# Twelve weight units of the second layer's token mixer get their lo part from an accumulating DMA and a negated ScalarE write

## The chip, the cores and the metric

One core of one Trainium2 chip runs the whole program. The metric is the device time of one execution in microseconds (us); the lower the better.

## What is computed

The reference is a decoder trunk of two layers over 256 tokens of width 1024, in float32. Each layer is a token mixer (one input projection of the normed activations, from which a latent attention, a second attention and a gated convolution are fed, then gates and an output projection) and a channel mixer:

```
z = h @ w_in
...
q_a = (rms_norm(q_lat, mla_q_norm_g) @ w_uq)...
kv = (rms_norm(kv_lat, mla_kv_norm_g) @ w_ukv)...
...
u = glu_a * jax.nn.sigmoid(glu_g)
u = causal_depthwise_conv(u, conv_dw_w, conv_dw_b)
u = jax.nn.silu(layer_norm(u, conv_ln_g, conv_ln_b))
...
merged = g[:, :, 0] * o_a + g[:, :, 1] * o_b + g[:, :, 2] * o_c
return merged @ w_out
```

In layer 2 (index 1 in the code) the change touches columns of `w_in` (those of the second attention's query, key and value, here called QKV, and those of the convolution's input, here called C) and the two up-projections `w_uq` (UQ) and `w_ukv` (UK).

## The kernel before

**Weights in units.** The weights stream from HBM in units of 128 x 1024 float32 (512 KB; 128 x 768 for UQ). SyncE (SP) issues one DMA for each into a tile `raw`, of which there are four (`wload`, L204). Every product is made from two parts of each operand: `hi`, the operand rounded to the matmul's fp32r type, and `lo`, the rest. `split` (L221 to L233) makes them for a weight unit: ScalarE copies `raw` into `hi` (tile `whi`, L231), and VectorE subtracts, `lo = raw - hi` (tile `wlo`, L232). There are four buffers of `whi` and of `wlo` as well. An activation's two parts are named `hh`/`hl`, `qlh`/`qll`, `klt` and so on.

**Three matmuls a product.** A product is hi times hi (L315), activation lo times weight hi (L316), activation hi times weight lo (L318). `flush` (L304) writes out a group of queued products: first the L315 and L316 matmuls of them all, then all the L318 matmuls. So `wlo` is needed only towards the end of a group; this last part is called phase 3 below. `take` (L280) keeps three units split ahead of the one in use. So `wlo` is written before the matmuls that come to need it.

**Order of the work.** The steps of a layer stand in a list written by hand (`STEPS`), one token for a step; a unit belongs to the step's token, and its load, its `hi` and its `lo` are written into the program when `take` draws it, three units ahead. Every engine then carries out its own instructions in the order in which the program's scheduler put them; the tiles rotate as they come free. SP's DMA queue is in order too: a load whose `raw` buffer isn't yet released holds up the loads behind it. The units of layer 2's mixer come in this order: QKV00, QKV01, the three of UQ (UQ0, UQ1, UQ2), QKV02, the two of UK (UK0, UK1), QKV03, QKV10 to QKV13, QKV20 to QKV23, C00, C01, C10, C11, C20, C21, then gate units (G) with C30 and C31 among them. Here QKVab is the b-th quarter of the inputs for the a-th of query, key, value, and Cab the b-th half for the a-th group of channels.

**What else runs there.** `proj_qkv` (L965) uses the QKV units one at a time. `up_q` (L987) takes all three UQ units and uses them in four groups of products; `up_kv` (L1002) takes the two UK units and does the same. Ahead of `up_q` ScalarE copies the latents out of PSUM (L926, L927, L929) and squares them (L938) for their norm. VectorE has, besides the subtractions, the 31 taps of the depthwise convolution in four groups of channels (L1141, `cacc`), spread over the steps from the first of the QKV group to the last of the second attention's steps, and the work on the attentions' queries and keys. After the last tap come the mean (a matmul on TensorE, L1154, tile `psb`) and its subtraction (L1159). GpSimd (POOL) does small powers for the norms (`rstd_of`, L536), and nothing else there.

Of the kernel before, what the change touches and what calls it, by code (L numbers as in the profile page):

```python
# [9 lines left out]
F32 = mybir.dt.float32  # L10
# [3 lines left out]
AF = mybir.ActivationFunctionType  # L14
ALU = mybir.AluOpType
# [42 lines left out]
LEAD = 16  # L58

LEADS = {(0, "O", 6): 0, (0, "G", 7, 0): 40, (1, "G", 6, 0): 0, (1, "O", 4): 40}  # L60
# [98 lines left out]
def trunk_kernel(ctx, tc, xT, crow, ccol, pos, invf, modb_d, cols_d, grow_d, wmh, wmr, wm, win1, wqkv,  # L159
                  wgc, wgab, wuq, wukv, woab, woc, wout, wup, wdn, out):  # L160
    nc = tc.nc
    te, ac, ve, gp, sy = nc.tensor, nc.scalar, nc.vector, nc.gpsimd, nc.sync
# [8 lines left out]
    def nm(s):  # L171
        uid[0] += 1
        return f"{s}_{uid[0]}"
# [27 lines left out]
    def wload(src, tag="raw", bufs=4):  # L201
        n = src.shape[1]
        t = wk.tile([P, 1024], F32, tag=tag, name=nm("raw"), bufs=bufs, align_bytes=LINE if tag != "raw" else None)
        sy.dma_start(t[:, 0:n], src)  # L204
        return t[:, 0:n]
# [11 lines left out]
    def wload_unit(src):  # L217
        loads[0] += 1
        return wload(src, *raw_tags[loads[0] % len(raw_tags)])

    def split(raw, lead):  # L221
        n = raw.shape[1]
        turn[0] += 1
        th, nh = hi_tags[turn[0] % len(hi_tags)]
        tl, nl = lo_tags[turn[0] % len(lo_tags)]
        hi, lo = (wk.tile([P, 1024 + 128], F32R, tag=t, name=nm(m), bufs=b, align_bytes=LINE)[:, lead:lead + n]
                  for t, m, b in ((th, "whi", nh), (tl, "wlo", nl)))
        with ExitStack() as es:
            for i in (pins.pop(0) if pins else hold[0] or []):
                es.enter_context(tc.issue_after(i))  # L230
            ac.activation(hi, raw, AF.Copy)  # L231
            ve.tensor_tensor(lo, raw, hi.bitcast(F32), op=ALU.subtract)  # L232
        return hi, lo  # L233

    def chop(src, n, c, size=1024):

        m = max(1, size // c)
        return [(src[:, k0 * c:min(n, k0 + m) * c], range(k0, min(n, k0 + m))) for k0 in range(0, n, m)]

    def token_units(l, t):  # L240

        if t[0] == "KL":
            return [(win1[l, t[1], :, 0:672], [0])]
        if t[0] == "QKV":
            return [chop(wqkv[l, t[1], t[2] // 2], 4, 512)[t[2] % 2]]
        if t[0] in ("UQ", "UK"):
            return chop(wuq[l], 3, 768) if t[0] == "UQ" else chop(wukv[l], 2, 1024)
        if t[0] in ("C", "G"):
            return [chop((wgc if t[0] == "C" else wgab)[l, t[1]], KD, S)[t[2]]]
        if t[0] == "O":  # L250
            return chop(woab[l, t[1]], 1, 1024)
        if t[0] == "OC" and t[1] % 2 == 0:
            return chop(woc[l, t[1] // 2], 1, 1024)
        if t[0] == "PR" and t[1] % 2 == 0:
            return chop(wout[l, t[1] // 2], 2, 1024)
        return []

    def all_units():
        for l in range(L):
            for k in range(KD):  # L260
                if l == 0:
                    yield win1[l, k, :, 0:672], [0], LEAD
                yield win1[l, k, :, 672:1696], [0], LEAD
            for t in CFG["order"][l]:
                yield from ((*u, LEADS.get((l, *t), LEAD)) for u in token_units(l, t))
            if l == 1:
                for first in (0, NRAW):
                    for i in range(2):
                        for j in range(first, first + NRAW):
                            yield *chop(wup[l, j], KD, S)[i], LEAD  # L270
            for up, j in FFN[l]:
                if up and l == 1 and j < 2 * NRAW:
                    continue
                for i, u in enumerate(chop(wup[l, j], KD, S) if up else chop(wdn[l, j], 1, 1024)):
                    yield *u, (0, 40)[i] if up and j in PAIRS else LEAD

    ahead = [AHEAD0]
    coming, ready = list(all_units())[::-1], []

    def take(n=1):  # L280

        while coming and len(ready) < n + ahead[0]:
            src, ks, lead = coming.pop()
            ready.append((split(wload_unit(src), lead), src.shape[1] // len(ks), ks))
        res = []
        for _ in range(n):
            (hi, lo), c, ks = ready.pop(0)
            res.append([(k, (hi[:, i * c:(i + 1) * c], lo[:, i * c:(i + 1) * c])) for i, k in enumerate(ks)])
        return res

    def take1():
        return take()[0][0][1]
# [486 lines left out]
    def layer(l):  # L779
# [65 lines left out]
        def pair(name, part, bank=psb):  # L845

            if part == 0:
                pairs[name] = bank()
            for k, w in take()[0]:
                cols2(pairs[name], w, k, k == 0, k == KD - 1)  # L850
            flush()
            return pairs[name]
# [114 lines left out]
        def proj_qkv(i, q):  # L967
            if q == 0:
                pqkv[i] = [psa() if i < 2 else psb() for _ in range(2)]
            pp = pqkv[i]  # L970
            for kk, w in take()[0]:
                k = 4 * (q // 2) + kk
                for b in range(NB):
                    rows(pp[b], w, k, b, k == 0, k == KD - 1)
            flush()
            if q < 3:
                return
            for b in range(NB):
                if i < 2:
                    if qks[b] is None:  # L980
                        qks[b] = mq()
                    ac.activation(qks[b][:, i * 512:(i + 1) * 512], pp[b], AF.Copy)
                else:
                    ac.activation(vb[:, b, :], pp[b], AF.Copy)
# [569 lines left out]
```

## Time and profile before

| what | value |
|---|---|
| runs of the kernel | 904.81, 904.56 and 902.16 us, median 904.56 us |
| the profiled execution | 905.91 us |
| its span, first to last instruction | 903.7 us |
| mean granted TensorE clock | 0.994 |
| weight units split | 286 |
| DMA traffic | 201.59 MB |

The profiled execution is 1.35 us above the median of the runs; the rest of its time beside the span, 2.2 us, lies ahead of the first and behind the last instruction. In the rows of the profile PE is a matmul on TensorE, PEld its weight load, DVE is VectorE, ACT is ScalarE, POOL is GpSimd and SP is SyncE. A row of a timeline is the start in us, the duration, the engine, the line, the operation, the tiles, and in brackets the idle time of the engine ahead of it with what ended it. In a row of groups the figures behind the first bar are busy us and mean ns of one instruction, and behind the second bar the idle time. Matmuls are pipelined, so a row's duration overlaps that of the next; how far apart rows start tells the pace.

### The profile page before, as it was taken

To read this page: it belongs to the slowest core of one execution; us is meant where nothing else is said; L and a number is where in the kernel's file an instruction comes from. 1 tells how busy PE (TensorE), PEld (TensorE's weight loads), DVE (VectorE), ACT (ScalarE), POOL (GpSimd) and SP (SyncE) were. 2 spreads that over 40 slices of the span, in tenths; PEclk is the share of its full clock that TensorE was granted. 3 is DMA by queue.
4 is the path that set the end of the run, shared out by engine and by line. 5 is a ranking of instruction groups with operands and counts; after the bars stand their busy time and mean duration, and the time that the engine had idled before them with its cause. 6 is when DMAs were issued, how large, how long until landed. Compare 5 with 4: busy or idle time off the path is not lost.

```text
span 903.7 us, 18611 instructions
## 1 busy us (share of the span) xinstructions
PE 884.4 (98%) x7247; PEld 839.6 (93%) x7247; DVE 808.1 (89%) x1592; ACT 559.3 (62%) x998; POOL 47.0 (5%) x36
## 2 busy tenths in 40 slices
PE   8999999999999999999999999999999999999998
PEld 6888888999997999999989988989999999999998
DVE  6989999999987999999774999999987899998774
ACT  4677588644755655556543676787465777556551
POOL 1010700000000000000000033000000000000000
PEclk8999999999999999999999999999999999999999
DMA  8956535699888889996652666156866576886631
GB/s 320 375 202 205 187 118 175 207 330 316 309 285 286 288 287 314 316 306 228 204 161 77 200 196 200 49 167 230 274 200 209 160 233 188 301 280 205 191 95 47
DMA packets 57976, 201.59 MB, mean 223 GB/s; under 512 B 6944, under 2 KB 8480, under 8 KB 57888
## 3 DMA queue, kind: packets, MB, share of 16 engines
q1 hardware_dynamic: 57888, 200.41, 66.5%
q8 instruction: 57, 0.93, 0.4%
q14 instruction: 31, 0.25, 0.1%
HBM read 199.33 MB, written 1.05 MB: 222 GB/s over the span
## 4 chain that ended last, share of the span: by engine, by line
PE 78%; DVE 11%; DMA 5%; ACT 3%; issue 2%; SPq 0%; POOL 0%; DVEq 0%; ACTq 0%; POOLq 0%
PE psb L315 16%; PE psb L316 15%; PE psb L318 15%; PE psa L315 8%; PE psa L316 8%; PE psa L318 8%; DVE wlo L232 3%; DVE cacc L1141 2%; ACT whi L231 1%; DVE raw L816 1%; PE psa L423 1%; PE psa L734 1%; PE psa L746 1%; DMA raw<-in_win 1%; DMA raw<-in_wmh 1%
## 5 line engine op out<-in xcount | busy, mean ns | idle before, releaser
L231 ACT ACTIVATE whi<-raw 128x1024 fp32r<-128x1024 f32 (+2 forms) x286 | 296.0, 1042 | 194.4 <-PE psb L316 98.5
L232 DVE TENSOR_TENSOR wlo<-raw,whi 128x1024 fp32r<-128x1024 f32 (+2 forms) x286 | 340.3, 1195 | 50.7 <-ACT whi L231 42.4
L315 PE MATMUL psb<-hh,whi 128*128 128x256 f32 x1056 | 256.0, 282 | 0.5 <-ACT p L713 0.3
L316 PE MATMUL psb<-hl,whi 128*128 128x256 f32 x1056 | 253.7, 280 | 0.0
L315 PEld LDWEIGHTS psb<-hh,whi 128*128 128x128 f32 x1056 | 198.9, 189 | 5.0 <-issue 2.6
L316 PEld LDWEIGHTS psb<-hl,whi 128*128 128x128 f32 x1056 | 199.0, 189 | 0.5 <-DVE wlo L232 0.4
L318 PE MATMUL psb<-hh,wlo 128*128 128x256 f32 x1056 | 145.0, 279 | 0.0
L318 PEld LDWEIGHTS psb<-hh,wlo 128*128 128x128 f32 x1056 | 131.7, 188 | 0.8 <-issue 0.8
L1141 DVE SCALAR_TENSOR_TENSOR cacc<-upad,cw,cacc 128x256 f32<-128x256 f32 x240 | 105.8, 478 | 0.4
L315 PE MATMUL psa<-mhl,whi 128*128 128x256 f32 x400 | 94.2, 278 | 0.0
L316 PE MATMUL psa<-mhl,whi 128*128 128x256 f32 x400 | 94.0, 278 | 0.0
L1423 DVE SCALAR_TENSOR_TENSOR e<-psb,fw,e 128x255 f32<-128x255 f32 (+1 forms) x168 | 80.0, 478 | 6.6 <-ACT e L1421 6.0
L536 POOL TENSOR_TENSOR rs<-rs,mhalf 128x8 f32<-128x8 f32 (+3 forms) x26 | 45.5, 1761 | 678.0 <-DVE rs L535 677.9
L315 PEld LDWEIGHTS psa<-mhl,whi 128*128 128x128 f32 x400 | 75.1, 188 | 0.0
L316 PEld LDWEIGHTS psa<-mhl,whi 128*128 128x128 f32 x400 | 75.0, 188 | 0.0
L406 DVE SCALAR_TENSOR_TENSOR raw<-raw,crow 128x1024 f32<-128x1024 f32 x56 | 68.3, 1220 | 0.9 <-DMA raw<-in_wmr 0.9
L1421 ACT ACTIVATE e<-psb,fb,fw 128x256 f32<-128x256 f32 x84 | 46.5, 554 | 23.6 <-DVE e L1423 20.1
L318 PE MATMUL psa<-mhl,wlo 128*128 128x256 f32 x400 | 54.0, 278 | 0.0
L318 PEld LDWEIGHTS psa<-mhl,wlo 128*128 128x128 f32 x400 | 49.5, 188 | 0.0
L1431 ACT ACTIVATE mhl<-e 128x256 fp32r<-128x256 f32 x44 | 18.4, 417 | 39.7 <-DVE e L1429 38.0
L315 PE MATMUL psb<-whi,hh 128*128 128x416 f32 (+1 forms) x96 | 30.9, 350 | 2.9 <-ACT hh L892 2.9
L315 PE MATMUL psa<-hh,whi 128*128 128x256 f32 x128 | 30.0, 281 | 0.0
(295 smaller groups left out, 1522.2 us busy)
## 6 DMA issues: line engine op xcount, KB each, us to landing
raw<-in_wup SPq DMA_DIRECT2D x88, 512.0 KB, 4.9
raw<-in_wmr SPq DMA_DIRECT2D x68, 512.0 KB, 5.4
raw<-in_wdn SPq DMA_DIRECT2D x44, 512.0 KB, 4.6
raw<-in_wgab SPq DMA_DIRECT2D x32, 512.0 KB, 5.0
raw<-in_wqkv SPq DMA_DIRECT2D x24, 512.0 KB, 4.7
raw<-in_wm SPq DMA_DIRECT2D x24, 512.0 KB, 4.7
raw<-in_win SPq DMA_DIRECT2D x16, 512.0 KB, 4.5
raw<-in_wgc SPq DMA_DIRECT2D x16, 512.0 KB, 4.4
```

The costliest lines, as they stand in the source:

```text
L231: ac.activation(hi, raw, AF.Copy)
L232: ve.tensor_tensor(lo, raw, hi.bitcast(F32), op=ALU.subtract)
L315: te.matmul(o, p1[0], p1[1], start=start, stop=False)
L316: te.matmul(o, p2[0], p2[1], start=False, stop=False)
L318: last = te.matmul(o, p3[0], p3[1], start=False, stop=stop)
L406: ve.scalar_tensor_tensor(raw, raw, scale, row, op0=ALU.mult, op1=ALU.mult, accum_out=acc)
L423: te.matmul(acc[32 * c:32 * c + 32, 0:S], cact[:, k:k + 1].to_broadcast([P, 32]), raw[:, c * S:(c + 1) * S], start=(k == 0), stop=(k == KD ...
L536: gp.tensor_tensor(r, r, mhalf[:, :n], op=ALU.pow)
L1141: ve.scalar_tensor_tensor(aj, upad[:, j, t:t + S], cw[:, j * 31 + t:j * 31 + t + 1], aj, op0=ALU.mult, op1=ALU.add)
L1421: ac.activation(t, src, AF.Identity, scale=fw[:, 2, c:c + 1], bias=fb[:, c:c + 1])
L1423: ve.scalar_tensor_tensor(t[:, d:S], src[:, 0:S - d], fw[:, 2 - d, c:c + 1], t[:, d:S], op0=ALU.mult, op1=ALU.add)
L1431: ac.activation(mh, th, AF.Copy)
```

## The change

For twelve units of layer 2's mixer (UQ1, UK1 and those of QKV and C with an odd second index: QKV01, QKV03, QKV11, QKV13, QKV21, QKV23, C01, C11, C21, C31), `lo` is made in another way. ScalarE writes minus the rounded weight into `lo` (`activation` with scale -1); GpSimd issues a DMA from `raw` to `lo`, which adds what it reads to what stands there; and ScalarE then writes `hi` as before. VectorE has no part in it. The other 274 units are made as before. The result is the same `lo`, and the matmuls are the same. Lines behind the first edit move by 5 to 9 (L318 becomes L327, L938 becomes L947).

```diff
-    def split(raw, lead):
+    def split(raw, lead, added=False):
...
-            ac.activation(hi, raw, AF.Copy)
-            ve.tensor_tensor(lo, raw, hi.bitcast(F32), op=ALU.subtract)
+            if added:
+                ac.activation(lo, raw, AF.Copy, scale=-1.0)
+                gp.dma_start(lo, raw, accum_op=ALU.add)
+                ac.activation(hi, raw, AF.Copy)
+            else:
+                ac.activation(hi, raw, AF.Copy)
+                ve.tensor_tensor(lo, raw, hi.bitcast(F32), op=ALU.subtract)
...
+    def added(l, t, i):
+
+        return l == 1 and (t[0] in ("UQ", "UK") and i % 2 == 1 or t[0] in ("QKV", "C") and t[2] % 2 == 1)
...
-                yield from ((*u, LEADS.get((l, *t), LEAD)) for u in token_units(l, t))
+                yield from ((*u, LEADS.get((l, *t), LEAD), added(l, t, i)) for i, u in enumerate(token_units(l, t)))
...
-            src, ks, lead = coming.pop()
-            ready.append((split(wload_unit(src), lead), src.shape[1] // len(ks), ks))
+            src, ks, lead, *how = coming.pop()
+            ready.append((split(wload_unit(src), lead, *how), src.shape[1] // len(ks), ks))
```

The scheduler orders each engine's instructions anew, and at three places this matters. The first is ScalarE ahead of the query up-projection; `raw_6737` (before) and `raw_6738` (after) hold UQ1, `ma` the latents.

```order
L231 ACTIVATE whi_6739<-raw_6737 128x768
L926 ACTIVATE ma_6717<-psb_6570 128x384
L927 ACTIVATE ma_6717<-psb_6572 128x256
L929 ACTIVATE kr_6720<-psb_6570 128x32
L926 ACTIVATE ma_6722<-psb_6571 128x384
L927 ACTIVATE ma_6722<-psb_6572 128x256
L929 ACTIVATE kr_6725<-psb_6571 128x32
L938 ACTIVATE b_1132_6728,lss_6727<-ma_6717 128x384
L938 ACTIVATE b_1140_6756,lss_6755<-ma_6722 128x384
```

The same place of the changed kernel:

```order
L234 ACTIVATE whi_6740<-raw_6738 128x768
L935 ACTIVATE ma_6718<-psb_6570 128x384
L936 ACTIVATE ma_6718<-psb_6572 128x256
L938 ACTIVATE kr_6721<-psb_6570 128x32
L935 ACTIVATE ma_6723<-psb_6571 128x384
L936 ACTIVATE ma_6723<-psb_6572 128x256
L938 ACTIVATE kr_6726<-psb_6571 128x32
L947 ACTIVATE b_1132_6729,lss_6728<-ma_6718 128x384
L232 ACTIVATE wlo_6741<-raw_6738 128x768
L947 ACTIVATE b_1132_6729,lss_6728<-ma_6718 128x256
```

The negated write of UQ1 (L232) stands behind its `hi` (L234), the six copies of the latents and one of the squares.

The second place is SP's queue of loads, with what each load waits for in brackets (DVE is VectorE, Activation is ScalarE, and DMAHW a load that landed earlier). Before, from QKV02's load to QKV10's; the two of `in_wukv` are UK0 and UK1, and the next is QKV03.

```order
L204 DMA raw_6806<-in_wqkv 128x1024 [waits DMAHW3_49,DVE_49]
L204 DMA raw_6812<-in_wukv 128x1024 [waits DMAHW4_49,DVE_49]
L204 DMA raw_6818<-in_wukv 128x1024 [waits DMAHW5_49,DVE_49]
L204 DMA raw_6870<-in_wqkv 128x1024 [waits DMAHW6_49,DVE_49,Activation_49]
L204 DMA raw_6888<-in_wqkv 128x1024 [waits DMAHW7_49,DVE_49]
```

The same loads in the changed kernel:

```order
L204 DMA raw_6808<-in_wqkv 128x1024 [waits DMAHW4_49,DVE_49]
L204 DMA raw_6814<-in_wukv 128x1024 [waits DMAHW3_49,DMASW0_49]
L204 DMA raw_6820<-in_wukv 128x1024 [waits DMAHW5_49,DMASW1_49,Activation_49]
L204 DMA raw_6873<-in_wqkv 128x1024 [waits DMAHW6_49,DVE_49]
L204 DMA raw_6892<-in_wqkv 128x1024 [waits DMAHW7_49,DVE_49]
```

DMASW0 is the accumulating DMA of QKV01 and DMASW1 that of UQ1: UK0's load now waits for the first and UK1's for the second, where both waited for a subtraction on VectorE.

The third place is TensorE in `up_kv`; `wlo_6815` and `wlo_6821` are the lo parts of UK0 and UK1 before. The last two matmuls of the first group of products and the second group:

```order
L318 MATMUL psb_6901<-wlo_6815,klt_6550 128x512
L318 MATMUL psb_6901<-wlo_6821,klt_6550 128x512
L315 MATMUL psb_6909<-whi_6814,klt_6550 128x512
L316 MATMUL psb_6909<-whi_6814,klt_6550 128x512
L315 MATMUL psb_6909<-whi_6820,klt_6550 128x512
L316 MATMUL psb_6909<-whi_6820,klt_6550 128x512
L318 MATMUL psb_6909<-wlo_6815,klt_6550 128x512
L318 MATMUL psb_6909<-wlo_6821,klt_6550 128x512
```

In the changed kernel the lo parts of UK0 and UK1 are `wlo_6817` and `wlo_6823`. Four L324 and L325 matmuls into `psb_6906` stand ahead of these rows:

```order
L327 MATMUL psb_6906<-wlo_6817,klt_6550 128x512
L324 MATMUL psb_6914<-whi_6816,klt_6550 128x512
L325 MATMUL psb_6914<-whi_6816,klt_6550 128x512
L324 MATMUL psb_6914<-whi_6822,klt_6550 128x512
L325 MATMUL psb_6914<-whi_6822,klt_6550 128x512
L327 MATMUL psb_6914<-wlo_6817,klt_6550 128x512
L324 MATMUL psb_6923<-whi_6816,klt_6550 128x512
L325 MATMUL psb_6923<-whi_6816,klt_6550 128x512
L324 MATMUL psb_6923<-whi_6822,klt_6550 128x512
L327 MATMUL psb_6906<-wlo_6823,klt_6550 128x512
L327 MATMUL psb_6914<-wlo_6823,klt_6550 128x512
L325 MATMUL psb_6923<-whi_6822,klt_6550 128x512
```

The first matmul that reads UK1's lo part stands 13 matmuls behind the first of this step (five before), since work of the next groups was moved ahead of it.

On GpSimd the twelve DMA issues stand among the powers (L536): QKV01's and UQ1's ahead of the two powers of the latents' norms, UK1's and QKV03's behind them, then one power of the queries' norm, QKV11's and QKV13's, and so on. On TensorE the matmul of the convolution's mean (L1154 before) stands one gate unit earlier.

## The prediction

> **What bounds the kernel now.** I read the page first. Its first and fourth parts:
>
> ```profile
> PE 884.4 (98%) x7247; PEld 839.6 (93%) x7247; DVE 808.1 (89%) x1592; ACT 559.3 (62%) x998; POOL 47.0 (5%) x36
> ...
> PE 78%; DVE 11%; DMA 5%; ACT 3%; issue 2%; SPq 0%; POOL 0%; DVEq 0%; ACTq 0%; POOLq 0%
> ```
>
> TensorE is busy 98% of the span and carries 78% of the chain that ended last; VectorE carries 11% of it. The change takes work from VectorE in one stretch, so I asked next for the busy time in slices of that stretch (columns: length, busy us and count for PE, PEld, DVE, ACT, POOL, then granted clock, DMA share, GB/s):
>
> ```profile
> 530.00:540.00 10.00, 10.00 (x45) 8.21 (x44) 10.00 (x21) 9.25 (x14) 7.08 (x3) 1.00 0.69 237
> 560.00:640.00 80.00, 77.93 (x682) 73.05 (x680) 78.58 (x160) 62.86 (x155) 2.15 (x2) 1.00 0.50 161
> 580.00:590.00 10.00, 10.00 (x93) 9.73 (x89) 10.00 (x20) 10.00 (x31) 0.00 (x0) 1.00 0.07 25
> ```
>
> VectorE has no free time here (10.00 of 10, 78.58 of 80), yet TensorE has nearly none either (77.93 of 80). A full VectorE costs time only where TensorE waits for it, so I asked for the waits from 556 to 640:
>
> ```profile
> PEld psb L1154 <- issue: 1.5, 1, 1.5
> PE psb L1154 <- DVE mod L407: 1.4, 1, 1.4
> PEld psb L315 <- ACT p L713: 0.5, 1, 0.5
> PEld psa L1051 <- issue: 0.5, 1, 0.5
> ...
> PEld psa L746 <- ACT qkTb L1052: 0.2, 1, 0.2
> ```
>
> TensorE waits once in this stretch for the end of VectorE's queue of taps and subtractions: at the convolution's mean (L1154), for 1.4 to 1.5 us. The two waits of 0.5 are attention work that goes back and forth between ScalarE and a full VectorE. By these rows a lighter VectorE can give back W = 1.5 + 0.5 + 0.5 = 2.5 us. It gives at least 1.4, if only L1154's wait goes, and at most 4.9, if all 12 rows of the weight load's waits go (from 1.5 down to the 0.2 of the last row shown; together 4.9). I take 2.5, which is also nearest to the 2.07 that TensorE is not busy in the 80 us from 560.
>
> **What goes from VectorE, and what comes to ScalarE.**
>
> ```profile
> L232 DVE TENSOR_TENSOR wlo<-raw,whi 128x1024 fp32r<-128x1024 f32 (+1 forms) x37 | 44.0, 1197 | 0.2 <-ACT whi L231 0.2
> 541.67 1.06 ACT L231 ACTIVATE whi<-raw 128x1024 fp32r<-128x1024 f32 x1 [1.55 <-PE psa L316]
> 512.39 0.85 ACT L231 ACTIVATE whi<-raw 128x768 fp32r<-128x768 f32 x1 [1.00 <-PE psb L316]
> ```
>
> From VectorE go 12 subtractions of 1.197 us, 14.4 us, against the 2.5 that TensorE can use: 11.9 us end as idle VectorE. ScalarE gets 12 more writes of the same form as `hi`: 11 x 1.06 + 0.85 = 12.5 us. It is 62.86 of 80 us busy in the last part, so most of this falls in its idle time; but between 580 and 590 it is busy 10.00 of 10 and feeds the attention that TensorE waits for (the L713 row). One negated write there would delay it by at most 1.05; most writes lie earlier. I take +0.5, ends 0 and 1.05.
>
> **What the DMA costs.** The new wait is the accumulating DMA: from the end of the negated write until `lo` has landed, X. The trace of before has no such DMA. The nearest rows are loads of the same size and, for the slope, a store of a quarter of it:
>
> ```profile
> raw<-in_wqkv SPq DMA_DIRECT2D x24, 512.0 KB, 4.7
> raw<-in_wgc SPq DMA_DIRECT2D x16, 512.0 KB, 4.4
> out_dram<-x SPq DMA_DIRECT2D x8, 128.0 KB, 1.9
> ```
>
> Low end: it costs no more than a load, 4.4. High end: it has to read its destination as well, another 512 KB; 384 KB more cost 4.7 - 1.9 = 2.8 us, so 512 KB cost 3.7, and 4.7 + 3.7 = 8.4. The two reads can overlap in part, so I take the middle, X = 6.5 (an estimate from these rows). The stall comes where phase 3 of an added unit begins earlier than X behind its negated write:
>
> ```profile
> 508.70 1.07 ACT L231 ACTIVATE whi<-raw 128x1024 fp32r<-128x1024 f32 x1 [0.78 <-PE psb L316]
> 514.57 0.57 ACT L938 ACTIVATE b<-ma 128x384 f32<-128x384 f32 x1
> 525.08 2.01 ACT L231 ACTIVATE whi<-raw 128x1024 fp32r<-128x1024 f32 x2
> 533.59 1.05 ACT L231 ACTIVATE whi<-raw 128x1024 fp32r<-128x1024 f32 x1
> 553.00 1.05 ACT L231 ACTIVATE whi<-raw 128x1024 fp32r<-128x1024 f32 x1
> ...
> 518.65 1.18 PE L318 MATMUL psa<-wlo,hh 128*128 128x512 f32 x4
> 520.70 0.51 PE L318 MATMUL psb<-wlo,qlh 128*128 128x384 f32 x2
> 528.65 0.39 PE L315 MATMUL psb<-whi,klt 128*128 128x512 f32 x1
> 528.88 0.39 PE L316 MATMUL psb<-whi,klt 128*128 128x512 f32 x1
> 541.47 1.07 PE L318 MATMUL psa<-wlo,hh 128*128 128x512 f32 x4
> 552.46 1.07 PE L318 MATMUL psb<-wlo,hh 128*128 128x512 f32 x4
> 570.13 1.11 PE L318 MATMUL psb<-hh,wlo 128*128 128x256 f32 x8
> ```
>
> - QKV01: `hi` starts at 508.70, two writes of 1.06 end by 510.8, phase 3 starts at 518.65: 7.8 us of slack, no stall at 6.5, 0.6 at 8.4, taken up below by UQ1's, which stands right behind.
> - UQ1: its `hi` starts at 512.39; in the new order the negated write stands behind the latents' copies and one square (514.57 + 0.57 = 515.1, less the overlap) and ends at 515.1 + 0.85 = 515.9. Its phase 3 is the second matmul of the row at 520.70, at 520.9: slack 5.0, stall X - 5.0 = 1.5.
> - UK1: in the new order 13 matmuls stand ahead of the first that reads its lo; they start 528.88 - 528.65 = 0.23 apart, so TensorE gets there at 528.65 + 13 x 0.23 = 531.6. ScalarE wrote UK0's and UK1's `hi` from 525.08 to 527.1; with the negated write, 528.1, and later by UQ1's stall, since the buffers that it writes come free behind UQ1's matmuls. Slack 3.5, stall X - 3.5 = 3.0. By SP's queue the same comes out: UK1's load now waits for UQ1's DMA, 515.9 + 6.5 = 522.4, plus the 4.7 to 5.0 of a load, two writes (2.1) and 6.5 more, 535.7 to 536.0, against 531.6 + 1.5 = 533.1: 2.6 to 2.9.
> - QKV03 has the stalls of both behind it on TensorE and is covered by them. QKV12's load waits for UK1's DMA now: 528.1 + 1.5 + 6.5 + 4.7 and its `hi`, 1.06, make 541.9; TensorE wants it behind QKV11's phase 3 (541.47 + 0.9, and 4.5 of stalls), at 546.9. Covered.
> - QKV11: `hi` 533.59 + 1.05, negated write to 535.7, phase 3 at 541.47: slack 5.8, stall X - 5.8 = 0.7. Both ends shift together with the stalls ahead.
> - QKV21: two writes from 541.67 end at 543.8, phase 3 at 552.46: 8.6. C01: 555.1 to 570.13: 15. The other QKV units lie as QKV21 does, the other C units as C01: no stall up to 8.4.
>
> Sum of the stalls: S = 1.5 + 3.0 + 0.7 = 5.2 at X = 6.5; 0.9 at 4.4; 3.4 + 4.9 + 2.6 = 10.9 at 8.4. TensorE is full at 530 to 540 now, so nothing there makes up for it, and the mean's wait comes 100 us later. VectorE goes on with its taps while TensorE waits, so the 2.5 remain.
>
> GpSimd's powers queue with the DMAs:
>
> ```profile
> 532.92 8.03 POOL L536 TENSOR_TENSOR rs<-rs,mhalf 128x16 f32<-128x16 f32 x3 [13.91 <-DVE rs L535]
> 535.68 2.00 ACT L231 ACTIVATE whi<-raw 128x1024 fp32r<-128x1024 f32 x2
> 541.75 0.69 DVE L1105 TENSOR_TENSOR ma<-kv,rs 128x512 f32<-128x512 f32 x1
> ```
>
> The second of the three powers (2.7 us each) now stands behind QKV13's DMA issue, and that behind QKV13's negated write: 537.7 + 1.06 + 5.2 of stalls = 544, so the power ends at 546.6, where VectorE uses it at 541.75 now, with taps queued behind. That can idle VectorE for up to 4.9 us. I price it at nothing: of the 14.4 us of relief 9.5 are left, and TensorE needs 2.5. Without that cover it would take back the whole 2.5.
>
> Total: 5.2 - 2.5 + 0.5 = +3.2. The profiled execution's 905.91 becomes 909.1; set against the median of the runs, 904.56, it is 907.8.
>
> [...]
>
> **The rivals.**
>
> 1. *Faster: the transfer is short.* With X at or under 4.4 only UK1 stalls, by 0.9 or less, and the relief stands: 904.56 + 0.5 - 2.5 = 902.6 with no stall, 904.56 + 0.5 - 4.9 = 900.2 if every wait of the stretch goes. It decides at X = 5.3, where S = 0.3 + 1.8 equals the 2.0 of net relief. For it: plain loads of this size land in 4.4 even with the queues 69% busy. Against it: the accumulate has to read twice.
>
> 2. *Slower: GpSimd's issue is held up by VectorE.* If GpSimd can't write what the DMA engines need while VectorE runs an instruction, each DMA waits for one of VectorE's instructions (1.2 us, and VectorE has no gap at 530 to 540): X = 7.7, S = 2.7 + 4.2 + 1.9 = 8.8, and 904.56 + 8.8 - 2.0 = 911.4. It decides from about X = 6.3, where the net passes 0.3%. For it: VectorE's solid rows. Against: no row shows GpSimd slowed. [...]
>
> 3. *Much slower: the transfers collide with the loads.* The loads keep the DMA engines 69% busy at 530 to 540. If the accumulating DMA gets only the 31% that they leave, its 3.7 us of reading last 3.7 / 0.31 = 12, and X is 10 or more: S = 5.0 + 6.5 + 4.2 at 10, and QKV13, QKV21 and QKV23, with some 8.6 of slack, add about 1.4 each, 19.9 in all: 904.56 + 19.9 - 2.0 = 922.5. It decides from X = 8.6. Against it: the loads themselves land in 4.7 at the same share.
>
> **How the numbers follow.** Under 0.3% of the time, 2.7 us, a measurement of this kernel can't be told from no change. The forecast, X from 5.3 to 8.4, has a chance of 0.45: slower by over 2.7 needs X above 6.3, 0.28 of it, the rest, 0.17, is the same within 2.7. Rival 1 has 0.33: 0.20 faster by more than 2.7 (W near its upper end), 0.13 the same. Rival 2 has 0.14 and rival 3 has 0.08, both slower. Together: faster 0.20, same 0.30, slower 0.50. The range runs from 900.5, near rival 1's 900.2, to 916, past the forecast's end (904.56 + 10.9 - 2.0 = 913.5) and rival 2 but short of rival 3. The forecast's own range is 904.6 to 913.5.
>
> **What would show each step.** In the changed kernel's waits from 515 to 545, TensorE (its weight load) should wait at L327 (L318 before) for the `wlo` that a DMA wrote: once at about 521 for 1.5 us, once at about 533 for 3.0, once at about 546 for 0.7. GpSimd's row of DMA issues should show some 6.5 us to landing. The wait at L1154 should be gone, and VectorE should show some 12 us of idle time between 556 and 640. The forecast is wrong if X is under 5.3, if the waits at L327 are absent although X is above 6, or if L1154 still waits.

## The result and the profile after

| what | before | changed |
|---|---|---|
| median of 11 runs each | 904.24 us | 909.34 us |
| the profiled execution, its span | 905.91 us, 903.7 us | 907.26 us, 905.5 us |

The changed kernel takes 1.0067 times as long as the one before (95% interval 1.0042 to 1.0092): 6.1 us more, with an interval from 3.8 to 8.3. The ratio goes by the fast runs alone, which leaves out one run of the kernel before, 917.04 us. The two profiled executions differ by 1.35 us only, and this needs care before anything is read from them. Here are three places of TensorE's timeline before: the last matmuls of QKV00, the first of C00, and the last of a gate unit behind the mean.

```profile
514.64 1.08 PE L318 MATMUL psa<-wlo,hh 128*128 128x512 f32 x4
...
562.28 0.36 PE L315 MATMUL psb<-hh,whi 128*128 128x256 f32 x1
...
660.55 1.12 PE L318 MATMUL psb<-hh,wlo 128*128 128x256 f32 x8
```

The same three in the changed kernel, and between them the rows in which TensorE waited for a lo part that a DMA wrote (UQ1, UK1, QKV11, QKV13 and QKV23, in this order):

```profile
507.92 1.08 PE L327 MATMUL psa<-wlo,hh 128*128 128x512 f32 x4
...
516.29 0.62 PE L327 MATMUL psb<-wlo,qlh 128*128 128x384 f32 x2 [0.96 <-DMA wlo<-raw]
529.52 0.73 PE L327 MATMUL psb<-wlo,klt 128*128 128x512 f32 x2 [2.20 <-DMA wlo<-raw]
540.22 1.21 PE L327 MATMUL psa<-wlo,hh 128*128 128x512 f32 x4 [0.44 <-DMA wlo<-raw]
546.24 1.20 PE L327 MATMUL psa<-wlo,hh 128*128 128x512 f32 x4 [0.23 <-DMA wlo<-raw]
559.31 1.70 PE L327 MATMUL psb<-wlo,hh 128*128 128x512 f32 x4 [1.80 <-DMA wlo<-raw]
...
565.39 0.37 PE L324 MATMUL psb<-hh,whi 128*128 128x256 f32 x1
...
661.94 1.12 PE L327 MATMUL psb<-hh,wlo 128*128 128x256 f32 x8
```

At QKV00 the changed execution is 6.72 us ahead (507.92 against 514.64); that lies in front of everything that the change touches. At the gate unit it is 1.39 behind. The stretch between the two takes 145.91 us before and 154.02 after: 8.1 us more. This **stage length** is what the traces are compared by from here on; each is that of a single execution. Up to C00 the loss is 9.8 us (57.47 against 47.64), and from there on 1.7 come back, the wait for the mean among them, which is gone from the list of waits. Counted from QKV00's last matmuls, TensorE is 0.9 us behind the kernel before at UQ's first matmuls, 2.3 behind UQ1's lo part, 5.5 at QKV11's, 6.0 at QKV13's, 8.1 at QKV23's and 9.8 at C00. Every step but the first (a wait for `qll`) and the last (the clock, below) ends at a late lo part.

The busy time in slices of the stretch shows it as well:

```profile
510.00:520.00 10.00, 8.17 (x43) 6.96 (x42) 9.22 (x30) 5.82 (x17) 2.24 (x3) 1.00 0.74 169
520.00:530.00 10.00, 7.80 (x37) 6.38 (x36) 8.63 (x19) 7.48 (x9) 1.81 (x2) 1.00 0.89 243
530.00:540.00 10.00, 9.78 (x43) 7.49 (x41) 7.13 (x19) 9.36 (x13) 5.04 (x4) 1.00 0.93 254
540.00:550.00 10.00, 9.56 (x40) 7.55 (x41) 7.02 (x15) 6.38 (x9) 7.19 (x4) 1.00 1.03 266
550.00:560.00 10.00, 8.20 (x36) 6.35 (x35) 9.48 (x21) 7.21 (x8) 4.84 (x5) 0.99 0.82 235
560.00:640.00 80.00, 79.49 (x681) 74.16 (x680) 67.33 (x135) 66.46 (x160) 7.95 (x7) 0.98 0.64 192
```

TensorE, busy before for all but 0.01 us between 510 and 560, now idles 6.5 us between 510 and 560 (8.17 + 7.80 + 9.78 + 9.56 + 8.20 of 50) and is fuller behind it (79.49 of 80 against 77.93). VectorE idles 8.5 us of the same 50: much of what it was spared is lost there. Between 560 and 640 it idles 12.7 us, near the 12 that the prediction gave as a sign. The DMA engines go from shares of 0.69 and 0.72 between 530 and 550 to 0.93 and 1.03.

Of the waits between 505 and 640, those of TensorE for UQ1, UK1 and QKV23 and for `qll`, and one of VectorE that is taken up below:

```profile
PEld psb L327 <- DMA wlo<-raw: 6.1, 3, 2.6
PE psb L327 <- DMA wlo<-raw: 5.0, 3, 2.2
DVE ma L1102 <- POOL rs L545: 2.8, 1, 2.8
PEld psb L955 <- DVE qll L958: 1.3, 1, 1.3
```

And the accumulating DMAs from issue to landing: those between 505 and 600 together, and by themselves QKV13's (issued at 538.8), QKV23's (551.7) and C21's (583.2).

```profile
wlo<-raw POOLq DMA_DIRECT2D x10, 512.0 KB, 5.8
...
wlo<-raw POOLq DMA_DIRECT2D x1, 512.0 KB, 7.4
...
wlo<-raw POOLq DMA_DIRECT2D x1, 512.0 KB, 7.6
...
wlo<-raw POOLq DMA_DIRECT2D x1, 512.0 KB, 4.5
```

One more thing is in the slices: the granted clock. Between 557 and 559 TensorE waits for QKV23, and then, though it has work, its clock is halved for some 3.4 us (0.57 on average over the 4 us of the second row):

```profile
557.00:559.00 2.00, 0.51 (x3) 0.08 (x1) 2.00 (x5) 0.99 (x2) 2.00 (x2) 1.00 0.69 211
559.50:563.50 4.00, 4.00 (x18) 3.36 (x18) 4.00 (x10) 2.87 (x5) 4.00 (x4) 0.57 0.78 214
```

From QKV23's last matmuls to C00's first, TensorE loses 1.75 us in this way (559.31 to 565.39 are 6.08; before, 557.95 to 562.28, 4.33).

### The profile page after: what moved, and what is told of

Same layout as the page of the kernel before. It is cut to its first block, busy times and chain, and to the rows that moved or that the text cites. A ratio compares the mean times of both kernels' runs of the same rounds, so it can differ in the third digit from the quotient of the medians.

```text
span 905.5 us, 18640 instructions
## 1 busy us (share of the span) xinstructions
PE 879.9 (97%) x7247; PEld 834.4 (92%) x7247; DVE 796.0 (88%) x1580; ACT 568.4 (63%) x1010; POOL 58.4 (6%) x48
## 4 chain that ended last, share of the span: by engine, by line
PE 76%; DVE 8%; DMA 7%; ACT 5%; issue 2%; SPq 0%; POOL 0%; DVEq 0%; ACTq 0%; POOLq 0%
PE psb L324 16%; PE psb L325 15%; PE psb L327 15%; PE psa L324 7%; PE psa L325 7%; PE psa L327 7%; DVE wlo L237 2%; DMA wlo<-raw 2%; ACT whi L236 2%; DVE raw L825 1%; PE psa L432 1%; DMA raw<-in_wqkv 1%; DVE cacc L1150 1%; PE psa L755 1%; ACT p L722 1%
## 5 line engine op out<-in xcount | busy, mean ns | idle before, releaser
L236 ACT ACTIVATE whi<-raw 128x1024 fp32r<-128x1024 f32 (+2 forms) x274 | 283.9, 1042 | 165.1 <-PE psb L325 84.0
L237 DVE TENSOR_TENSOR wlo<-raw,whi 128x1024 fp32r<-128x1024 f32 (+2 forms) x274 | 325.7, 1193 | 57.2 <-ACT whi L236 48.6
L324 PE MATMUL psb<-hh,whi 128*128 128x256 f32 x1056 | 254.4, 282 | 1.0 <-DVE e L1432 0.4
L325 PE MATMUL psb<-hl,whi 128*128 128x256 f32 x1056 | 251.9, 279 | 0.0
L324 PEld LDWEIGHTS psb<-hh,whi 128*128 128x128 f32 x1056 | 198.5, 188 | 6.0 <-issue 3.9
L325 PEld LDWEIGHTS psb<-hl,whi 128*128 128x128 f32 x1056 | 198.6, 188 | 0.7 <-DVE wlo L237 0.4
L327 PE MATMUL psb<-hh,wlo 128*128 128x256 f32 x1056 | 144.5, 278 | 0.0
L327 PEld LDWEIGHTS psb<-hh,wlo 128*128 128x128 f32 x1056 | 131.3, 188 | 0.6 <-issue 0.6
L324 PE MATMUL psa<-mhl,whi 128*128 128x256 f32 x400 | 93.5, 277 | 0.0
L325 PE MATMUL psa<-mhl,whi 128*128 128x256 f32 x400 | 93.2, 277 | 0.0
L324 PEld LDWEIGHTS psa<-mhl,whi 128*128 128x128 f32 x400 | 74.9, 188 | 0.0
L325 PEld LDWEIGHTS psa<-mhl,whi 128*128 128x128 f32 x400 | 74.9, 188 | 0.0
L327 PE MATMUL psa<-mhl,wlo 128*128 128x256 f32 x400 | 53.6, 276 | 0.0
L327 PEld LDWEIGHTS psa<-mhl,wlo 128*128 128x128 f32 x400 | 49.2, 188 | 0.0
L324 PE MATMUL psb<-whi,hh 128*128 128x416 f32 (+1 forms) x96 | 30.9, 349 | 4.9 <-ACT hh L901 4.9
L325 PE MATMUL psb<-whi,hl 128*128 128x416 f32 (+1 forms) x96 | 29.6, 344 | 0.2 <-DVE hl L902 0.2
```

Of the source, the lines that this page charges most:

```text
L324: te.matmul(o, p1[0], p1[1], start=start, stop=False)
L325: te.matmul(o, p2[0], p2[1], start=False, stop=False)
L327: last = te.matmul(o, p3[0], p3[1], start=False, stop=stop)
```

## The experiments

Theory A at the outset was the prediction's: TensorE waits for lo parts that land late, at few units near their use. Theory B: the extra writes on ScalarE delay what else it does. Theory C: the transfers slow the weight loads. Each run was timed against the kernel before, in five rounds. The last two columns are the ratio with its interval and the stage length in the run's profile, minus that of before.

| run | what it is | ratio | stage |
|---|---|---|---|
| (changed) | all twelve units | 1.0067 (1.0042 to 1.0092) | +8.1 |
| e1_c_only | only the four C units | 0.9997 (0.9978 to 1.0015) | -0.7 |
| e2_proj_only | only QKV, UQ, UK | 1.0129 (1.0104 to 1.0155) | +12.5 |
| e3_vec_add | VectorE adds raw, no DMA | 1.0057 (1.0037 to 1.0077) | +4.0 |
| e4_no_dma | no DMA, no addition | 1.0043 (1.0017 to 1.0069) | +5.8 |
| e5_short | DMA of 64 columns | 1.0057 (1.0035 to 1.0080) | +6.4 |
| e6_pin_no_dma | e4, preparation pinned | 1.0045 (1.0026 to 1.0064) | +5.5 |
| e7_up_only | only UQ1, UK1 | 1.0039 (1.0019 to 1.0059) | +4.0 |
| e8_pin | changed, preparation pinned | 1.0091 (1.0061 to 1.0121) | +8.9 |
| e9_ms_vec_add | e3, squares moved ahead | 1.0007 (0.9986 to 1.0028) | +1.3 |
| e10_ms_changed | changed, squares moved ahead | 1.0131 (1.0112 to 1.0149) | +12.9 |
| e11_ms_before | before, squares moved ahead | 0.9997 (0.9980 to 1.0013) | +0.3 |
| e12_ms_no_dma | e4, squares moved ahead | 1.0049 (1.0032 to 1.0067) | +3.5 |

**The parts by themselves.** Only the C units:

```diff
-        return l == 1 and (t[0] in ("UQ", "UK") and i % 2 == 1 or t[0] in ("QKV", "C") and t[2] % 2 == 1)
+        return l == 1 and t[0] == "C" and t[2] % 2 == 1
```

> Only the four C units keep the accumulating DMA; the eight of QKV, UQ and UK get their lo from VectorE again. Theory A (TensorE waits for lo parts that land too late, and only at UQ1, UK1, QKV11, QKV13 and QKV23): no wait at L327 for a lo that a DMA wrote, the wait for the mean at L1163 gone by the 4.8 us that VectorE is spared, so 1 to 2.5 us faster than before (ratio 0.997 to 0.999). Theory B (the extra writes on ScalarE delay what it does for TensorE): a third of the loss, +2 us. Theory C (the transfers' traffic slows the weight loads): a third of it as well, +2 us, with waits of ScalarE for raw.

It is level with before. No wait at L327 for a DMA and no wait for the mean are left, as theory A has it, but the gain is not there: the relief is worth 0.7 us in the stage, and the interval reaches from 2.0 us faster to 1.4 slower.

Only the other eight units:

```diff
+        return l == 1 and (t[0] in ("UQ", "UK") and i % 2 == 1 or t[0] == "QKV" and t[2] % 2 == 1)
```

> Only the eight units of QKV, UQ and UK keep the accumulating DMA; the C units are as before. Theory A: all of the stalls are still there, about 8 us by the trace of the changed kernel (2.3 around UQ1, 2.6 at UK1, 0.7 at QKV11, 0.5 at QKV13, 1.8 at QKV23 and as much behind it), and the wait for the mean shrinks as before, so +5 to +7 us (ratio 1.006 to 1.008). Theories B and C: two thirds of the loss, +4 us.

This loses 11.6 us, more than the whole change, and more than any of the theories gave. Its list of waits has the late lo parts, and others beside them:

```profile
PEld psb L327 <- DMA wlo<-raw: 5.6, 3, 2.6
...
PEld psa L743 <- ACT p L734: 2.6, 2, 1.5
...
PEld psa L1131 <- ACT qkT L1132: 2.0, 2, 1.8
PEld psa L688 <- ACT p L722: 1.8, 1, 1.8
```

TensorE waits for the first attention too (`qkT` and `p`, which ScalarE writes). Late lo parts don't explain these by themselves.

**Without the DMA.** ScalarE still writes minus the rounded weight, and VectorE adds raw (first), or nothing adds it (second):

```diff
-                gp.dma_start(lo, raw, accum_op=ALU.add)
+                ve.tensor_tensor(lo, raw, lo.bitcast(F32), op=ALU.add)
```

```diff
-                gp.dma_start(lo, raw, accum_op=ALU.add)
```

> All twelve units: ScalarE writes minus the rounded weight into lo as in the changed kernel, but VectorE adds raw to it in place of the DMA. ScalarE has its twelve extra writes, VectorE its twelve instructions as before, and no transfer runs. Theory A: no stall at L327 for a DMA; within 0.3% of before, at most +1 us for lo that comes one ScalarE write later. Theory B: the whole loss stays, +5 to +6 us. Theory C: 0.

> All twelve units: ScalarE's extra write stays, neither a DMA nor VectorE adds raw. It leaves out the addition of raw for twelve units, so their lo is minus hi. It shows what the relief of VectorE is worth when nothing has to be waited for. Theory A: 1.5 to 2.5 us faster than before (ratio 0.997 to 0.9985), the wait at L1163 gone. Theory B: still slower by 4 to 6 us. Theory C: as A.

Theory A fails as the sole cause: with no accumulating DMA at all, 5.1 and 3.9 us of loss stay. Theory C has no part in them, as these transfers are gone. In e3 the loss lies at the attention again:

```profile
PEld psa L1131 <- ACT qkT L1132: 1.6, 2, 1.4
PEld psa L688 <- ACT p L722: 1.4, 1, 1.4
```

**A short DMA, a pinned order, and two units alone.** In e5 only 64 columns are added; in e6 and e8 the second attention's preparation, which VectorE did 10 us earlier in the changed kernel, counted from QKV00's last matmuls (L1049 from 561.12, 53.2 behind them; before, L1040 from 578.19, 63.5 behind them), is kept behind the first attention's softmax bound `nb`; e7 has only UQ1 and UK1.

```diff
+                gp.dma_start(lo[:, 0:64], raw[:, 0:64], accum_op=ALU.add)
...
-            ve.tensor_scalar(nb, mx, -scale, None, op0=ALU.mult)
+            lastnb[:] = [ve.tensor_scalar(nb, mx, -scale, None, op0=ALU.mult)]
...
         def moba_prep(b):
+            with tc.issue_after(lastnb[0].ins) if l == 1 else ExitStack():
+                moba_prep_(b)
...
+        return l == 1 and t[0] in ("UQ", "UK") and i % 2 == 1
```

> The changed kernel, but each of the twelve DMAs adds only the first 64 columns of 1024 (768); the rest of those lo parts stays minus hi. The order of the instructions is that of the changed kernel nearly to the row, the transfer is a sixteenth. Theory A (TensorE waits for late lo parts): if X is mostly transfer, the waits at L327 shrink to under 1 us and what is left is what the run without a DMA showed, ratio 1.004; if X is mostly a fixed price, X stays above 4.5 and the ratio above 1.0055. Theory D (the new order itself costs, since the time that VectorE is spared was filled with work of later steps): at least 1.004 in either case.

> The run without a DMA (lo of twelve units is minus hi, the addition is left out), and the second attention's preparation in layer 2 (L1049 and what follows on VectorE) is kept behind the softmax bound nb of the first attention's second group, as before the change. Theory D: the 3 us that TensorE waited for the first attention's p goes, and the halved clock behind it; 3.5 to 4.5 us less than without the pin, ratio 0.998 to 1.0005. If the extra writes of ScalarE are the cause: no change, 1.004.

> Only UQ1 and UK1 keep the accumulating DMA. Theory A: these two alone bring the waits at L327 that they bring in the changed kernel, 1.3 and 2.6 us, with 0.9 ahead of them, so +4 to +5 us (ratio 1.004 to 1.0055). Theory D: little is spared on VectorE, so little moves: 0 to +1 us.

> The changed kernel whole, with the second attention's preparation kept behind the first attention's nb as in the run above. Theory A with the order's cost hidden behind the stalls: the same as the changed kernel, ratio 1.006 to 1.0075, since TensorE is late already and the waits for p are 0.3 us there. If the order's cost adds to the stalls: 1.002 to 1.004.

The transfer is most of X: 32 KB land in 2.4 us in the median, against 5.8 for 512 KB in the changed kernel, and one wait of 1.0 at L327 is left in e5.

```profile
PE psb L327 <- DMA wlo<-raw: 1.0, 1, 1.0
...
wlo<-raw POOLq DMA_DIRECT2D x12, 32.0 KB, 2.4
```

But its ratio, 1.0057, stays: the waits for `qkT` and `p` appear in their place (2.1 and 2.2 us). The pin changes nothing in e6 (1.0045 against 1.0043); why this doesn't clear the order is said below. With it e8 isn't better than the changed kernel: 1.0091, above both values that were expected. In e7 UQ1's DMA landed in 4.1 us and TensorE didn't wait for it; UK1's wait made most of the loss, and what followed made it larger:

```profile
530.24 1.22 PE L327 MATMUL psb<-wlo,klt 128*128 128x512 f32 x2 [2.20 <-DMA wlo<-raw]
...
532.00:533.50 1.50, 1.50 (x5) 1.11 (x5) 0.12 (x1) 1.03 (x2) 1.34 (x1) 0.52 0.91 235
```

After 2.2 us of waiting the clock is at 0.52. Up to C00 this run loses 4.9 us: 0.8 in a wait for `qll`, and the rest mainly by UK1's stall and the half clock. Behind C00 0.9 come back.

**ScalarE's squares.** What is common to e3 and e4 shows on ScalarE. The norms of the first attention need the squares of the queries (L1075 before, L1084 after), for two blocks of tokens. Before:

```profile
529.35 0.84 ACT L1075 ACTIVATE ma<-ma 128x768 f32<-128x768 f32 x1
...
532.86 0.83 ACT L1075 ACTIVATE ma<-ma 128x768 f32<-128x768 f32 x1
```

In e3, with ScalarE's busy time of that slice (the fourth engine column):

```profile
531.50 0.86 ACT L1084 ACTIVATE ma<-ma 128x768 f32<-128x768 f32 x1
540.55 0.88 ACT L1084 ACTIVATE ma<-ma 128x768 f32<-128x768 f32 x1
...
530.00:540.00 10.00, 10.00 (x45) 8.19 (x45) 8.37 (x17) 10.00 (x15) 3.00 (x1) 1.00 0.59 204
```

ScalarE is full, the scheduler put writes for later weight units ahead of the second square, and it comes late: 26.8 us behind QKV00's last matmuls, against 18.2 before. The norm's sum on VectorE, the power on GpSimd, the preparation and the softmax all follow from it. Theory E is therefore that the extra writes cost through these squares. The test moves the two steps that make them ahead by one to four unit steps, in four kernels, that of before among them:

```diff
- UQ QKV02 UK QKV03 MS0 QKV10 QKV11 v0 QKV12 MS1 QKV13
+ UQ QKV02 UK MS0 MS1 QKV03 QKV10 QKV11 v0 QKV12 QKV13
```

> As the run in which VectorE adds raw (no transfer, ScalarE's twelve extra writes stay), and the step that squares the first attention's queries and keys on ScalarE (MS0, MS1) stands ahead of the QKV03 step, so that the square of the second block runs some 6 us earlier, ahead of the writes of later units. Theory E (ScalarE is full between 524 and 544 and its extra writes push these squares back by 8 us; norms, preparation and softmax come late, and TensorE waits for qkT and p from 558 on): most of the 5.2 us goes, ratio 0.999 to 1.002. If the waits of 558 to 580 have another origin: no change, 1.0055.

> The changed kernel whole, with MS0 and MS1 moved ahead in the same way. In the changed kernel TensorE waits little for qkT and p, since the late lo parts hold it up first; theory A: those stalls (about 6 us and the halved clock) stay, ratio 1.0055 to 1.0075. If ScalarE's squares were the only cause: 0.999 to 1.002.

> The kernel before, with MS0 and MS1 moved ahead: the control for the move by itself. Both theories: the same as before within 0.2%.

> As the run without a DMA and without the addition (lo of twelve units is minus hi, the addition of raw is left out), with MS0 and MS1 moved ahead. It shows what the spared VectorE time is worth when neither a transfer nor the squares hold anything up. Theory E: 1.5 to 2.5 us faster than before, ratio 0.9975 to 0.9985; at most 1.0005 if the 0.9 us at UQ1 stays. If not: 1.004.

The second square of e9 starts at 531.45, 22.1 us behind QKV00's last matmuls, and the loss goes from 1.0057 to 1.0007; moved in the kernel before, the steps do nothing (0.9997). So e3's loss hangs on where these two steps stand, as theory E has it.

It doesn't hold for e12, which differs from e9 only in that VectorE doesn't add raw: with less to do, it is slower by 0.42% (1.0049 against 1.0007). Its waits, on ScalarE and TensorE:

```profile
PE psa L687 <- ACT p L721: 2.8, 1, 2.8
ACT p L721 <- DVE nb L705: 2.6, 1, 2.6
```

TensorE waits for `p`, `p` for `nb`, and `nb` stands in VectorE's queue. Here is the time from QKV00's last matmuls to this first `nb` of layer 2, in e9, in e12 and in e6 (VectorE is the third engine column):

```profile
509.39:565.83 56.44, 56.44 (x308) 49.04 (x307) 56.41 (x121) 46.69 (x74) 28.13 (x10) 1.00 0.56 185
...
510.45:571.95 61.50, 59.67 (x324) 51.19 (x322) 56.68 (x133) 47.12 (x74) 18.80 (x10) 1.00 0.51 171
...
509.93:572.14 62.21, 59.69 (x324) 51.20 (x322) 56.89 (x137) 47.12 (x74) 25.51 (x10) 1.00 0.51 168
```

VectorE works 56.4 us ahead of `nb` in e9 and 56.7 in e12, although nine instructions on weight units are spared there: the scheduler filled the time. In the order of before, of e3 and of e9, 67 of the 124 conv taps stand ahead of this `nb`, and nothing of the second attention's preparation; in the changed kernel, in e4 and in e12 there are 82 taps and nine instructions of the preparation (6.2 us), which nobody waits for yet. That `nb` is 5.1 us later in e12 comes with 4.8 us of idle time: VectorE waits for powers of GpSimd (3.9 us in two pieces at L1101, 0.7 at L1115), and with the spared time filled up nothing makes up for it. Behind the last of these waits stand the nine instructions of the preparation and only three taps more than in e9. All this is read from the traces; no run held back both the taps and the preparation. e6 held back the preparation alone, and the scheduler put 14 more taps in its place (96 ahead of `nb`), so that VectorE works (56.9 us) and idles (5.3) as in e4 (56.7 and 5.3). So e6 doesn't show that the order is harmless.

And e10, expected level with the changed kernel, is worse (1.0131). The move brought GpSimd's powers ahead of QKV13's DMA:

```profile
541.08 1.06 ACT L232 ACTIVATE wlo<-raw 128x1024 fp32r<-128x1024 f32 x1
...
541.95 5.29 POOL L545 TENSOR_TENSOR rs<-rs,mhalf 128x16 f32<-128x16 f32 x2 [1.12 <-DVE rs L544]
547.20 0.90 POOL L233 DMA_DIRECT2D wlo<-raw  x1
...
552.24 1.20 PE L327 MATMUL psa<-wlo,hh 128*128 128x512 f32 x4 [2.88 <-DMA wlo<-raw]
```

The negated write ends at 542.1, two powers hold the queue until 547.2, and TensorE waits 2.9 us at a unit that cost 0.2 in the changed kernel. Not all of e10's loss is this wait: QKV11 costs 1.4 there, against 0.4, and TensorE waits 1.7 us for `qkT` and 0.9 for `p`.

## Why the prediction was right, and where it was not

The direction and the mechanism named first were right: 907.8 was forecast, 3.2 us more; 6.1 (3.8 to 8.3) were measured, inside the range of 900.5 to 916.0 but nearly twice the forecast's loss.

- **X.** Forecast 6.5, from 4.4 to 8.4; the ten DMAs have a median of 5.8 from issue to landing, from 4.5 to 7.6, and 0.3 to 0.4 lie between the end of a negated write and the issue (UK1 to QKV23), so X was some 6.1 to 6.2. Rival 1, the short transfer, is out: no DMA of that size was under 4.5 in the changed kernel, UK1's in e7 took 5.6, and three of e10 took 6.9, 6.9 and 5.0. Rival 2 is out too: GpSimd's issuing rows take 0.94 us at 551.71, where VectorE has no gap (8.00 of 8 from 551 to 559), and 0.88 at 612.75, where it is busy for 5.25 of 10. X goes with the traffic, though not strictly: 7.4 and 7.6 where the DMA share is 0.82 to 1.03, 4.5 at 583, where it is 0.40 (582 to 586), but 5.6 for UK1, where it is 0.89. No run varied the traffic alone, so it was not shown that this is rival 3's collision at a smaller size. Set against the 2.4 for 32 KB of e5, the 5.8 for 512 KB are 3.4 us more: beside loads and with an addition, the part that grows with the bytes is the larger here. How much of it is the reading of the destination, no run shows.
- **UQ1, UK1, QKV11.** Forecast 1.5, 3.0 and 0.7, together 5.2; the waits were 0.96, 2.20 and 0.44 by TensorE's rows, and by the places of the matmuls TensorE lost 1.4 at UQ1 and 3.2 from there to QKV11's lo part, together 4.6. These terms stand.
- **QKV23.** "The other QKV units lie as QKV21 does" is a step that failed. Its negated write stands behind its `hi` and two other copies and ends at 551.29 (550.23 + 1.06), 6.2 us ahead of phase 3 and not 8.6, and its DMA took 7.6. The wait was 1.80. By the places of the matmuls TensorE lost 2.1 us there. (QKV13, forecast free as well, waited 0.23 and cost 0.5.)

```profile
548.30 1.07 ACT L234 ACTIVATE whi<-raw 128x1024 fp32r<-128x1024 f32 x1 [0.56 <-DMA raw<-in_wqkv]
549.28 1.06 ACT L991 ACTIVATE mq<-psa 128x512 f32<-128x512 f32 x2
550.23 1.06 ACT L232 ACTIVATE wlo<-raw 128x1024 fp32r<-128x1024 f32 x1
```

- **The clock.** No term of the sum had it: 1.75 us behind QKV23.
- **ScalarE, "+0.5".** Taken by itself this is the step that was wrong by most, though in the changed kernel the late lo parts cover it. I priced the extra writes where ScalarE was 10.00 of 10 late in the stretch, and passed over the 9.25 of 10 of the row at 530 to 540; six of the twelve writes fall between 520 and 552 (UK1 to QKV23). Alone, they cost 5.1 us (e3), and by e9 nearly all of it hangs on the place of the steps with the squares.
- **The relief, 2.5.** L1154's wait went, and 1.7 us came back behind C00 all in all, against 2.0 net in the forecast. But "VectorE goes on with its taps while TensorE waits" was half the truth: the spared time went to 15 taps and to the second attention's preparation ahead of the softmax, VectorE waited 2.8 us for a power at L1102, and sparing VectorE cost time (e12 against e9). That wait isn't the one that was priced at nothing, behind a DMA in GpSimd's queue. GpSimd was idle and began the power as soon as VectorE had written its input, and VectorE had next to nothing else to do for the 2.95 us that it takes; before, 3.2 us of other work, a subtraction among it, lay between:

```profile
530.44 2.95 POOL L545 TENSOR_TENSOR rs<-rs,mhalf 128x16 f32<-128x16 f32 x1 [4.21 <-DVE rs L544]
...
533.42 0.69 DVE L1102 TENSOR_TENSOR ma<-ma,rs 128x512 f32<-128x512 f32 x1 [2.81 <-POOL rs L545]
```

- **GpSimd's queue.** The power that was feared to come late, behind QKV13's DMA, cost VectorE no wait at the second L1102 (548.93) and 0.6 us at L1114, so the price of nothing was nearly right. The other way round, DMAs that stand behind powers, I didn't look at, and e10 shows its price.
- **UQ's `qll`.** The 0.9 us in front of UQ1, a wait for VectorE's `qll`, had no term either. It is in every profiled run that has UQ1's write on ScalarE with less on VectorE (0.7 to 0.9 us), and not in e3 and e9; why VectorE is later with `qll` there stays open.
- **Why it came out near all the same.** The causes don't add. While the late lo parts hold TensorE up, `p` and `qkT` have time to get ready: in the changed kernel TensorE waits no more than 0.6 us at a time for them. Take the DMA away (e4) or make it short (e5), and they become the bound. By ratios, the changed kernel's 1.0067 stands against 1.0043 without the DMA's waits and 1.0039 with UK1's and UQ1's almost alone. In the trace 4.6 of the 9.8 us lost up to C00 stand in the sum's terms; the other 5.2 (0.9 ahead of UQ1, 0.5 at QKV13, 2.1 at QKV23, 1.75 of clock) stand in none. That the measured time lies inside the range owes to the range's width, and in part to luck.

## What to carry to other kernels

Before moving work to an engine that is idle on average, read its busy share in the slices where the moved instructions fall, and find which of its other instructions feed the bounding engine there. Work taken from a full engine is worth only what the new order does with the time; count what moved ahead of the instruction that the bound waits for, and the waits that the relieved engine then runs into. When two ways of losing lie in a row, undoing one shows the other: undo each alone before giving either the whole loss.

## What the hardware showed

TensorE's clock was halved after waits of three us and less, for about 3.4 us each time: after 1.8 (QKV23 in the changed kernel), 2.2 (UK1 in e7) and 3.0 (for `p` in e4, where the slice below follows it). After UK1's 2.2 us in the changed kernel it was not: the clock is at 1.00 from 529 to 533. Nor was it after 2.9 in e10 (QKV13), where the matmuls behind the wait start 0.23 us apart, as ahead of it; in e7's halved stretch they start 0.43 apart.

```profile
578.50:581.50 3.00, 3.00 (x16) 3.00 (x16) 3.00 (x8) 3.00 (x9) 0.00 (x0) 0.50 0.00 0
```

So of two waits of 2.2 us one is followed by the halved clock and one isn't, and a wait of 1.8 us is followed by it where one of 2.9 isn't.

The halved stretch of the changed kernel runs from 559.8 to 563.2 (the clock is at 0.98 from 559.6 to 559.8, at 0.50 from there to 563.2, and at 0.98 again up to 563.4). Here are the 3.41 us ahead of it, and a stretch of the same length that reaches into UK1's wait:

```profile
556.38:559.79 3.41, 1.61 (x7) 1.01 (x7) 3.41 (x9) 1.61 (x2) 3.21 (x2) 1.00 0.66 196
525.66:529.07 3.41, 1.67 (x8) 1.02 (x6) 3.41 (x8) 1.96 (x3) 0.57 (x1) 1.00 1.06 216
```

TensorE was busy for 1.61 us of the first and the clock was halved behind it; it was busy for 1.67 us of the second and nothing followed. UK1's wait of 2.2 us runs on past the end of the second stretch, so it counts there only in part. In e10 TensorE is busy for 1.6 us of a stretch of that length (547.74 to 551.15; its last matmul there ends at 549.36), and nothing followed. Neither the length of a wait nor the busy time of such a stretch tells by itself whether the clock is halved; what does, no run here shows.
